# A hybrid encoder block on one Trainium2 core: backward GLA contributions copied by VectorE, the last head's second norm and the MLP's low parts placed later

## The chip, the core and the metric

The kernel runs on one core of one Trainium2 chip. The metric is the device time of one execution in microseconds. Five engines work side by side, each through its own queue in order: TensorE (PE; its weight loads are shown as PEld), VectorE (DVE), ScalarE (ACT), GpSimd (POOL) and SyncE (SP), which issues most DMA transfers. TensorE accumulates in PSUM, where the kernel keeps four pairs of tiles (banks) of 128 x 512 float32 values, tagged "mm", "s", "o" and "t".

## The reference

One encoder layer on 1024 tokens of width 1024, in float32:

```python
n = rmsnorm(h, ln_mix_g)
proj = n @ w_in                      # q/k/v for attention, q/k/v/r and decay factors for GLA
y_na = neighbourhood_attention(...)  # 8 heads x 64, window 8 x 16 on a 16 x 64 grid, softmax with bias
y_gla = bidirectional_gla(...)       # 4 heads, chunks of 64 tokens, forward + backward state
h = h + concat([y_na, y_gla]) @ w_out
h = h + square(relu(rmsnorm(h, ln_ff_g) @ w1)) @ w2
return rmsnorm(h, ln_final_g)
```

For each GLA head a chunk contributes k^T v to a state in each direction; the states of the 16 chunks follow from the contributions by a scan, `S = decay * S + contribution`, forward in 64 partitions and backward in the other 64. The output of a head is the sum of a product within the chunk (masked scores times v) and a product of the decayed q with the state. It is then normed over the head's 128 values and multiplied by a gate.

## The kernel before

All activations lie transposed, features in partitions, in two halves of 512 tokens (`hf`). Float32 products are made of float32r parts: a value is split into a high part (a rounded copy by ScalarE) and a low part (value minus high part, a subtraction), and a product is three matmuls: high x high, high x low, low x high.

The stages follow each other: the input's norm and first projections; four GLA heads; attention in four pairs of heads (`p`), each in eight column blocks (`b`); the output projection; the MLP in four chunks of the hidden width, of which the first is done plainly (`FirstPlain`, `SecondPlain`) and the next by seven products of sums of blocks (`First`, `Second`, Strassen's scheme); the last chunk together with the final norm. Projections that a later stage needs are cut into steps of three matmuls (`Fill`), which are put between the parts of GLA and attention by tables of step counts (`GLA_FILL`, `NA_FILL`), so that TensorE has work while the other engines prepare. Their weights come by SP (`wf`); ScalarE makes a negated copy, a DMA from POOL's queue adds the weights to it (`wl`), and ScalarE casts the high part (`wh`).

The order on each engine is a static one. A scheduler orders instructions by dependencies, priorities (`tc.high_priority`) and its own estimate of times. `tc.keep_in_program_order` (`kp` in the MLP) pins an instruction behind all that was traced before on its engine. In the MLP all is pinned, so the code's order is the engines' order.

*A GLA head* (lines 670 to 693). `gla_contrib` (L569) makes the contributions of eight chunks into two banks tagged "s" and copies them to the state tile `st`: the forward half, partitions 0 to 63, by L583, the backward half, partitions 64 to 127, by L586, both on ScalarE; that is four copies for each of two calls. `gla_scan` runs the scan on VectorE, L606 forward and L609 backward, first steps 1 to 7 (not pinned), then 8 to 11 behind `gla_within(h, 0)`, then 12 to 14 behind `gla_within(h, 1)`. `gla_within` makes the scores within the chunks into two "s" banks (of two in all) and copies them masked by VectorE (L600). `gla_gates` of the next head uses "s" banks too (tile `la`). `gla_norm` (L629) norms one half: a sum over partitions by TensorE into a "t" bank, then in `rstd_from` Ln, Exp, Identity and Square on ScalarE (L230, L231, L237, L238) and two steps on VectorE (L239, L240), then the gate (L635) and the head's output (L636), which still lies in an "o" bank.

*The start of attention* (L890 to L897). The bias of the first pair is loaded and masked (`bias_for`, `masked`, L771), eight steps of filler run, then `softmax(0, 0)` is made: scores into two "s" banks, per head of the pair an addition of the bias with a maximum on VectorE (L825), an exponential with its sum on ScalarE (L827), a reciprocal and a scaling on VectorE (L829, L830). `softmax` of the next block needs the same two banks. `turn` transposes the result (L120, tile `pt`).

*The first MLP products.* `prepare(k)` queues, ahead of product k, what is due: the high and low part of the weights of product k + 2 (`prep2`), the activation of product k - 1 (`acts`), and jobs from a table. Products 0 to 7 work on the first token half, 8 to 15 on the second, 16 on are the second matmul. The jobs make the normed input of the second half (`normed`, L1377, eight values at products 2 to 7) and the sums of blocks that the later chunks need (`sums123`, L1386, at products 8 to 15; `sum4`, L1398, at 33 to 40). `put` (L1369) splits a value: a rounded copy on ScalarE (L1371), then the low part on VectorE (`low`, L1056). `whole` (L1365) adds high and low part on GpSimd.

Of the kernel before, what the change touches and what calls it, by code (L numbers as in the profile page):

```python
# [18 lines left out]
P = 128  # L19
# [48 lines left out]
def block_kernel(ctx, tc, xT, g_mix, w_in, w_z, rpb, na_mask, gu, gb, g_gla, sel_f, sel_b,  # L68
# [390 lines left out]
    with pool("gla", R) as gp:  # L459
# [110 lines left out]
        def gla_contrib(h, kt, st, hf):  # L570
            cb = [bank("s", f"c{h}_{hf}_{i}") for i in range(2)]
            for i in range(8):
                n = hf * 8 + i
                o = 64 * (n % 2)
                PE.matmul(cb[n % 2][:, (i // 2) * P:(i // 2 + 1) * P],
                          kt[o:o + 64, n // 2, :], vtok[h][o:o + 64, n // 2, :],
                          start=True, stop=True)
            for par in range(2):
                src = cb[par].rearrange("p (a b) -> p a b", a=4)
                n0 = hf * 8 + par  # L580

                k = 4 if n0 + 7 < NCH else 3
                S.copy(st[0:64, n0 + 1:n0 + 2 * k:2, :], src[0:64, 0:k, :])  # L583

                k = 0 if n0 > 0 else 1
                S.copy(st[64:128, n0 - 1 + 2 * k:n0 + 6:2, :], src[64:128, k:4, :])  # L586

        def gla_within(h, hf, qD, kI):

# [39 lines left out]
        def gla_norm(h, hf, ob, sq):  # L629
            c = slice(hf * H, (hf + 1) * H)  # L630
            v = bank("t", f"ov{h}_{hf}")
            PE.matmul(v, ones, sq, start=True, stop=True)
            r = rstd_from(v, 1.0 / P, gp, "n", H, "g1", 2)
            if (h, hf) in gated:
                V.tensor_tensor(r, yg[h][:, c], r, op=ALU.mult)  # L635
            V.tensor_tensor(yg[h][:, c], r, ob, op=ALU.mult)  # L636
            normed.add((h, hf))
# [22 lines left out]
        for h in range(GH):  # L660
# [12 lines left out]
            gla_scan(dec, st, 1, NCH // 2)  # L673
            fill.at(GLA_FILL, h, 3)
            gla_within(h, 0, qD, kI)
            gla_scan(dec, st, NCH // 2, NCH - 4)
            fill.at(GLA_FILL, h, 4)
            gla_within(h, 1, qD, kI)
            gla_scan(dec, st, NCH - 4, NCH - 1)
            fill.at(GLA_FILL, h, 5)  # L680
            if h + 1 < GH:
                bs[h + 1] = gla_gates(h + 1)
# [7 lines left out]
            fill.at(GLA_FILL, h, 9)  # L690
            gla_norm(h, 0, ob[0], sq[0])
            fill.at(GLA_FILL, h, 10)
            gla_norm(h, 1, ob[1], sq[1])
        bias_rows(range(ROWS))
        fill.run()
    gla_stack.close()
# [38 lines left out]
    with soon("na") as ap, soon("qkv") as qp:  # L735
# [154 lines left out]
        qt = lambda: qp.tile([P, H], F32, tag="qt", name="qt", bufs=2)  # L890
        qk = qk_tiles(0)
        fill.add(na_v(0), ("v", 0))
        with tc.high_priority(offset=SOON_B):
            bt = bias_for(0)
        fill.run(NA_PRE)
        xs = softmax(0, 0, *qk, bt)
        masked(bt, (5, 0))  # L897
        for p in range(NH // 2):
            if p > 1:
# [273 lines left out]
    class Second(Stage):  # L1173
# [61 lines left out]
        def add(self, p, j, o, s):  # L1235
            for d, c0 in {1: ((j, 0),), 5: ((j + 4, H),), 6: ((j, H),), 3: ((j, H),),
                          7: ((j + 4, H),), 2: ((j, 0),), 4: ((j + 4, 0),)}[p]:
                c = slice(c0 + s.start, c0 + s.stop)
                kp(V.tensor_tensor(hT[:, d, c], hT[:, d, c], o[:, s], op=ALU.add))  # L1239

    class FirstPlain(Stage):

        order = [((hf, m), kh) for hf in range(2) for m in range(4) for kh in range(2)]

        def __init__(self, c):
            self.w, self.u, self.parts = Weights(w1[c], ("A11", "A12", "A21", "A22")), {}, {}

        def prep2(self, p, kh):
            self.parts[p, kh] = self.w.low(self.w.high(f"A{p[1] // 2 + 1}{kh + 1}", p[1] % 2))

        def mm(self, p, kh):
            (hf, m), w = p, self.parts.pop((p, kh))
# [114 lines left out]
        kp(G.tensor_tensor(dst, h.bitcast(F32), l.bitcast(F32), op=ALU.add))  # L1367

    def put(key, k, x):  # L1369
        h, l = place(key, k)  # L1370
        kp(S.copy(h, x))  # L1371
        low(l, x, h, V)

    b = {}

    def normed(key, k):
        c = {"B12": 0, "B22": 1}[key]  # L1377
        if k == 0 and "S" not in b:
            b["S"] = mu.tile([P, D], F32, tag="S", name="b0")
        b[key, k] = t = (b["S"][:, c * H:(c + 1) * H] if k == 0 else  # L1380
                         mp.tile([P, H], F32, tag=("uh", "ul")[c], name=f"b{c}{k}", bufs=3))
        kp(V.scalar_tensor_tensor(t, hT[:, 4 * c + k, H:T], gff[:, 4 * c + k:4 * c + k + 1], r1,
                                  op0=ALU.mult, op1=ALU.mult))
        put(key, k, t)

    def sums123(k, step):  # L1386
        b12, b22 = b["B12", k], b["B22", k]
        if step == 0:
            b["B11", k] = ub("b11")
            whole(b["B11", k], "B11", k)  # L1390
            kp(V.tensor_tensor(b22, b22, b12, op=ALU.subtract))
            put("T3", k, b22)
        else:
            kp(V.tensor_tensor(b12, b12, b["B11", k], op=ALU.subtract))
            kp(V.tensor_tensor(b22, b22, b["B11", k], op=ALU.add))
            put("T1", k, b12)
            put("T2", k, b22)

    def sum4(k, step):
        if step == 0:  # L1400
            b["x", k] = x = [mp.tile([P, H], F32, tag=tag, name=f"b4{k}", bufs=3) for tag in ("uh", "ul")]
            whole(x[0], "B21", k)
            whole(x[1], "T2", k)
        else:
            x = b["x", k]
            kp(V.tensor_tensor(x[0], x[0], x[1], op=ALU.subtract))
            put("T4", k, x[0])

    for n, k in enumerate((2, 3, 3, 4, 5, 5, 6, 7)):
        job(k, normed, ("B12", "B22")[n // 4], n % 4)  # L1410
    for n, k in enumerate((1, 2, 3, 0)):
        for step in range(2):
            job(8 + 2 * n + step, sums123, k, step)
    for k in range(4):
        for step in range(2):
            job(33 + 2 * k + step, sum4, k, step)

    f2 = SecondPlain(0, f1.u)
    stage(f2)
# [165 lines left out]
```

## Time and profile before

| | |
|---|---|
| time, median of 3 runs | 1180.3 us (1179.51 to 1181.38) |
| the profiled execution | 1180.51 us |
| its span, first to last instruction | 1178.6 us |
| TensorE busy | 1149.7 us, 98% |
| VectorE busy | 862.7 us, 73% |
| ScalarE busy | 664.8 us, 56% |
| GpSimd busy | 241.6 us, 21% |
| mean granted clock of TensorE | 0.990 |

Busy time is the time in which an engine has an instruction in work. [...] In a timeline, the number in brackets is how long the engine stood idle before the instruction, and behind the arrow stands what it waited for.

### The profile page before, as it was taken

To read this page: it belongs to the slowest core of one execution; us is meant where nothing else is said; L and a number is where in the kernel's file an instruction comes from. 1 tells how busy PE (TensorE), PEld (TensorE's weight loads), DVE (VectorE), ACT (ScalarE), POOL (GpSimd) and SP (SyncE) were. 2 spreads that over 40 slices of the span, in tenths; PEclk is the share of its full clock that TensorE was granted. 3 is DMA by queue.
4 is the path that set the end of the run, shared out by engine and by line. 5 is a ranking of instruction groups with operands and counts; after the bars stand their busy time and mean duration, and the time that the engine had idled before them with its cause. 6 is when DMAs were issued, how large, how long until landed. Compare 5 with 4: busy or idle time off the path is not lost.

```text
span 1178.6 us, 15430 instructions
## 1 busy us (share of the span) xinstructions
PE 1149.7 (98%) x5632; PEld 945.6 (80%) x5632; DVE 862.7 (73%) x1565; ACT 664.8 (56%) x1222; POOL 241.6 (21%) x199
## 2 busy tenths in 40 slices
PE   8999899999999999999999999999999999999996
PEld 8878788767887878887788888888888888888876
DVE  8777868766767785686858875967859768587455
ACT  6767566656666665455634636446355463453665
POOL 5200000202021123510003320402304114032005
PEclk8999999989999999999999999999999999999998
DMA  7333132322324252320211112111211122111204
GB/s 241 76 86 94 41 72 46 87 69 55 80 45 100 68 179 73 107 107 8 82 54 36 54 54 72 37 55 54 72 66 31 50 69 72 54 37 54 72 1 143
DMA packets 40283, 84.03 MB, mean 71 GB/s; under 512 B 9264, under 2 KB 20656, under 8 KB 40208
## 3 DMA queue, kind: packets, MB, share of 16 engines
q1 hardware_dynamic: 36608, 71.11, 18.1%
q0 software_dynamic: 3456, 11.94, 5.8%
q8 instruction: 44, 0.72, 0.2%
q14 instruction: 31, 0.25, 0.1%
q10 hardware_dynamic: 144, 0.00, 0.0%
HBM read 78.85 MB, written 5.96 MB: 72 GB/s over the span
## 4 chain that ended last, share of the span: by engine, by line
PE 83%; DVE 7%; ACT 6%; issue 1%; DMA 1%; SPq 0%; DVEq 0%; ACTq 0%
PE f L115 26%; PE u L115 24%; PE proj L115 15%; PE op L115 7%; PE sc L115 2%; PE no L115 2%; PE o L115 1%; PE pt L120 1%; PE sb L115 1%; PE ob L115 1%; PE z L115 1%; PE a L115 1%; DMA wl<-in_w_in 1%; PE c L115 1%; PE opl L115 0%
## 5 line engine op out<-in xcount | busy, mean ns | idle before, releaser
L1079 ACT CAST ph<-A 128x512 fp32r<-128x512 f32 x166 | 102.9, 621 | 146.5 <-PE f L115 73.6
L1057 POOL TENSOR_TENSOR ul<-uB,uh 128x512 fp32r<-128x512 f32 x84 | 109.1, 1317 | 330.5 <-ACT uh L1092 213.4
L115 PE MATMUL f<-uh,ph 128*128 128x512 f32 x400 | 155.9, 390 | 2.1 <-ACT u L1100 1.4
L115 PE MATMUL f<-ul,ph 128*128 128x512 f32 x400 | 155.8, 390 | 0.1
L115 PE MATMUL f<-uh,pl 128*128 128x512 f32 x400 | 155.8, 389 | 0.0
L1057 DVE TENSOR_TENSOR pl<-A,ph 128x512 fp32r<-128x512 f32 x166 | 112.7, 688 | 52.6 <-ACT ph L1079 52.6
L115 PE MATMUL proj<-nh,wh 128*128 128x512 f32 x352 | 151.1, 429 | 0.0
L115 PE MATMUL proj<-nh,wl 128*128 128x512 f32 x352 | 139.4, 396 | 1.4 <-DMA wl<-in_w_in 1.4
L115 PE MATMUL proj<-nl,wh 128*128 128x512 f32 x352 | 138.9, 395 | 0.0
L1239 DVE TENSOR_TENSOR hT<-hT,f 128x512 f32<-128x512 f32 x168 | 113.0, 687 | 19.8 <-PE f L115 19.6
L115 PEld LDWEIGHTS f<-uh,ph 128*128 128x128 f32 x400 | 75.1, 188 | 18.4 <-ACT u L1100 1.8
L115 PEld LDWEIGHTS f<-ul,ph 128*128 128x128 f32 x400 | 75.1, 188 | 16.0 <-DVE ul L1057 0.4
L115 PEld LDWEIGHTS f<-uh,pl 128*128 128x128 f32 x400 | 75.1, 188 | 15.6
L115 PE MATMUL u<-n,ph 128*128 128x512 f32 x288 | 85.2, 391 | 0.0
L115 PEld LDWEIGHTS proj<-nh,wh 128*128 128x128 f32 x352 | 67.2, 191 | 18.2 <-issue 5.6
L1092 ACT CAST uh<-uB 128x512 fp32r<-128x512 f32 x84 | 51.9, 618 | 51.1 <-PE f L115 33.0
L115 PEld LDWEIGHTS proj<-nh,wl 128*128 128x128 f32 x352 | 66.8, 190 | 16.9 <-DMA wl<-in_w_in 1.8
L115 PE MATMUL u<-T,ph 128*128 128x512 f32 x256 | 77.0, 390 | 0.2 <-ACT ph L1079 0.2
L115 PEld LDWEIGHTS proj<-nl,wh 128*128 128x128 f32 x352 | 67.2, 191 | 11.7 <-issue 1.7
L115 PE MATMUL op<-y,wh 128*128 128x512 f32 x240 | 75.6, 396 | 0.4 <-DVE y L714 0.4
L115 PE MATMUL u<-nt,ph 128*128 128x512 f32 x224 | 69.0, 389 | 0.0
L827 ACT ACTIVATE xsc<-xsc,sm 128x384 f32<-128x384 f32 (+1 forms) x64 | 37.3, 584 | 51.3 <-DVE sm L825 51.1
(302 smaller groups left out, 2469.6 us busy)
## 6 DMA issues: line engine op xcount, KB each, us to landing
A<-in_w SPq DMA_DIRECT2D x64, 512.0 KB
wf<-in_w_in SPq DMA_DIRECT2D x22, 512.0 KB
wl<-in_w_in POOLq DMA_DIRECT2D x21, 512.0 KB, 6.7
wf<-in_w_out SPq DMA_DIRECT2D x17, 512.0 KB
hT<-in_xT SPq DMA_DIRECT2D x2, 2048.0 KB
xs<-in_xT SPq DMA_DIRECT2D x6, 512.0 KB
out<-hT SPq DMA_DIRECT2D x4, 512.0 KB
out<-hT SPq DMA_DIRECT2D x8, 256.0 KB
```

The source lines that it names most:

```text
L115: m = nc.tensor.matmul(*args, **kw)
L120: tc.keep_in_program_order(nc.tensor.transpose(*args, **kw))
L827: S.activation(x[:, :n], x[:, :n], AF.Exp, scale=-1.0, bias=sm[:, i, 0:1], accum_out=sm[:, i, 1:2])
L1057: return kp(eng.tensor_tensor(l, x, h.bitcast(F32), op=ALU.subtract))
L1079: kp(S.copy(ph, x))
L1092: kp(S.copy(uh, x))
L1239: kp(V.tensor_tensor(hT[:, d, c], hT[:, d, c], o[:, s], op=ALU.add))
```

## The change

In `gla_contrib` the copy of the backward half goes from ScalarE to VectorE. In the head's loop `gla_scan` now runs steps 8 and 9 before the second `gla_within`, and 10 to 14 behind it. For the last head the second `gla_norm` isn't called; its sum over partitions stays, its ScalarE steps are traced ahead of the bias load of attention, into tiles of attention's pool (`qc`, `qt`), and its four VectorE steps behind `softmax(0, 0)`, the first of them pinned there.

In the MLP low parts are no longer subtracted at once: `put`, and `prep2` of `FirstPlain` from product 2 on, note them in a list, and `settle` subtracts what is owed, after the next value has been made. The jobs of `normed` and `sums123` start one product earlier, in part, and go through k = 0, 1, 2, 3. `sums123` no longer calls `whole`: it subtracts the high and the low part one after the other on VectorE, and T2 is made from T1.

```diff
--- before.py
+++ after.py
@@ -583,7 +583,7 @@
                 S.copy(st[0:64, n0 + 1:n0 + 2 * k:2, :], src[0:64, 0:k, :])
 
                 k = 0 if n0 > 0 else 1
-                S.copy(st[64:128, n0 - 1 + 2 * k:n0 + 6:2, :], src[64:128, k:4, :])
+                V.tensor_copy(st[64:128, n0 - 1 + 2 * k:n0 + 6:2, :], src[64:128, k:4, :])
 
         def gla_within(h, hf, qD, kI):
 
@@ -673,10 +673,10 @@
             gla_scan(dec, st, 1, NCH // 2)
             fill.at(GLA_FILL, h, 3)
             gla_within(h, 0, qD, kI)
-            gla_scan(dec, st, NCH // 2, NCH - 4)
+            gla_scan(dec, st, NCH // 2, NCH // 2 + 2)
             fill.at(GLA_FILL, h, 4)
             gla_within(h, 1, qD, kI)
-            gla_scan(dec, st, NCH - 4, NCH - 1)
+            gla_scan(dec, st, NCH // 2 + 2, NCH - 1)
             fill.at(GLA_FILL, h, 5)
             if h + 1 < GH:
                 bs[h + 1] = gla_gates(h + 1)
@@ -690,7 +690,13 @@
             fill.at(GLA_FILL, h, 9)
             gla_norm(h, 0, ob[0], sq[0])
             fill.at(GLA_FILL, h, 10)
-            gla_norm(h, 1, ob[1], sq[1])
+            if h + 1 < GH:
+                gla_norm(h, 1, ob[1], sq[1])
+            else:
+                v_last = bank("t", "ovlast")
+                PE.matmul(v_last, ones, sq[1], start=True, stop=True)
+                o_last = ob[1]
+                assert (h, 1) in gated
         bias_rows(range(ROWS))
         fill.run()
     gla_stack.close()
@@ -890,10 +896,22 @@
         qt = lambda: qp.tile([P, H], F32, tag="qt", name="qt", bufs=2)
         qk = qk_tiles(0)
         fill.add(na_v(0), ("v", 0))
+
+        ly = qp.tile([P, T], F32, tag="qc", name="ly")[:, 0:H]
+        lt, lu = qt(), qt()
+        S.activation(lt, v_last, AF.Ln, bias=epsb, scale=LNSH / P)
+        S.activation(ly, lt, AF.Exp, bias=expb, scale=-0.5)
+        S.activation(lu, v_last, AF.Identity, bias=epsn, scale=-0.5 / P)
+        S.activation(lt, ly, AF.Square)
         with tc.high_priority(offset=SOON_B):
             bt = bias_for(0)
         fill.run(NA_PRE)
         xs = softmax(0, 0, *qk, bt)
+        tc.keep_in_program_order(V.tensor_tensor(lt, lt, lu, op=ALU.mult))
+        V.scalar_tensor_tensor(ly, lt, 1.5, ly, op0=ALU.add, op1=ALU.mult)
+        c = slice(H, T)
+        V.tensor_tensor(ly, yg[GH - 1][:, c], ly, op=ALU.mult)
+        V.tensor_tensor(yg[GH - 1][:, c], ly, o_last, op=ALU.mult)
         masked(bt, (5, 0))
         for p in range(NH // 2):
             if p > 1:
@@ -1238,15 +1256,24 @@
                 c = slice(c0 + s.start, c0 + s.stop)
                 kp(V.tensor_tensor(hT[:, d, c], hT[:, d, c], o[:, s], op=ALU.add))
 
+    owed = []
+
     class FirstPlain(Stage):
 
         order = [((hf, m), kh) for hf in range(2) for m in range(4) for kh in range(2)]
+        late_lows = False
 
         def __init__(self, c):
             self.w, self.u, self.parts = Weights(w1[c], ("A11", "A12", "A21", "A22")), {}, {}
 
         def prep2(self, p, kh):
-            self.parts[p, kh] = self.w.low(self.w.high(f"A{p[1] // 2 + 1}{kh + 1}", p[1] % 2))
+            ph, x = self.w.high(f"A{p[1] // 2 + 1}{kh + 1}", p[1] % 2)
+            pl = mp.tile([P, H], F32R, tag="pl", name="pl", bufs=3)
+            self.parts[p, kh] = ph, pl
+            if self.late_lows:
+                owed.append((pl, x, ph))
+            else:
+                low(pl, x, ph, V)
 
         def mm(self, p, kh):
             (hf, m), w = p, self.parts.pop((p, kh))
@@ -1367,9 +1394,14 @@
         kp(G.tensor_tensor(dst, h.bitcast(F32), l.bitcast(F32), op=ALU.add))
 
     def put(key, k, x):
+
         h, l = place(key, k)
         kp(S.copy(h, x))
-        low(l, x, h, V)
+        owed.append((l, x, h))
+
+    def settle():
+        while owed:
+            low(*owed.pop(0), V)
 
     b = {}
 
@@ -1381,23 +1413,29 @@
                          mp.tile([P, H], F32, tag=("uh", "ul")[c], name=f"b{c}{k}", bufs=3))
         kp(V.scalar_tensor_tensor(t, hT[:, 4 * c + k, H:T], gff[:, 4 * c + k:4 * c + k + 1], r1,
                                   op0=ALU.mult, op1=ALU.mult))
+        settle()
         put(key, k, t)
 
     def sums123(k, step):
         b12, b22 = b["B12", k], b["B22", k]
+        h, l = place("B11", k)
         if step == 0:
-            b["B11", k] = ub("b11")
-            whole(b["B11", k], "B11", k)
+            x = ub("t3")
+            kp(V.tensor_tensor(x, b22, b12, op=ALU.subtract))
+            settle()
+            put("T3", k, x)
+            kp(V.tensor_tensor(b12, b12, h.bitcast(F32), op=ALU.subtract))
+        else:
+            kp(V.tensor_tensor(b12, b12, l.bitcast(F32), op=ALU.subtract))
+            settle()
+            put("T1", k, b12)
             kp(V.tensor_tensor(b22, b22, b12, op=ALU.subtract))
-            put("T3", k, b22)
-        else:
-            kp(V.tensor_tensor(b12, b12, b["B11", k], op=ALU.subtract))
-            kp(V.tensor_tensor(b22, b22, b["B11", k], op=ALU.add))
-            put("T1", k, b12)
+            settle()
             put("T2", k, b22)
 
     def sum4(k, step):
         if step == 0:
+            settle()
             b["x", k] = x = [mp.tile([P, H], F32, tag=tag, name=f"b4{k}", bufs=3) for tag in ("uh", "ul")]
             whole(x[0], "B21", k)
             whole(x[1], "T2", k)
@@ -1406,14 +1444,17 @@
             kp(V.tensor_tensor(x[0], x[0], x[1], op=ALU.subtract))
             put("T4", k, x[0])
 
-    for n, k in enumerate((2, 3, 3, 4, 5, 5, 6, 7)):
+    f1.late_lows = True
+    for n, k in enumerate((2, 2, 3, 3, 4, 5, 5, 6)):
         job(k, normed, ("B12", "B22")[n // 4], n % 4)
-    for n, k in enumerate((1, 2, 3, 0)):
+    for k in range(4):
         for step in range(2):
-            job(8 + 2 * n + step, sums123, k, step)
+            job(7 + 2 * k + step, sums123, k, step)
+    job(15, settle)
     for k in range(4):
         for step in range(2):
             job(33 + 2 * k + step, sum4, k, step)
+    job(41, settle)
 
     f2 = SecondPlain(0, f1.u)
     stage(f2)
```

## Rows read from the trace of the kernel before

**Rows 1.** The page, part 1: busy us, share of the span, instructions.

```profile
PE 1149.7 (98%) x5632; PEld 945.6 (80%) x5632; DVE 862.7 (73%) x1565; ACT 664.8 (56%) x1222; POOL 241.6 (21%) x199
```

**Rows 2.** Stretch, its us; busy us of PE, PEld, DVE, ACT, POOL; PEclk; DMA share, GB/s.

```profile
115.00:128.00 13.00, 11.26 (x80) 8.55 (x78) 8.29 (x19) 9.87 (x16) 0.86 (x1) 0.97 0.39 97
128.00:140.00 12.00, 10.53 (x51) 7.85 (x52) 9.96 (x23) 3.82 (x7) 0.00 (x0) 0.90 0.17 49
250.00:265.00 15.00, 12.12 (x43) 8.47 (x42) 11.59 (x32) 6.85 (x16) 0.86 (x1) 0.77 0.32 69
548.00:585.00 37.00, 33.53 (x140) 25.55 (x139) 30.43 (x46) 24.87 (x44) 3.07 (x2) 1.00 0.21 68
```

**Rows 3.** The chain that ended last, one full-pace piece: start, us, what.

```profile
621.96 38.09 PE u L115 x168
```

**Rows 4.** Timeline of head 1: start, us, engine, line, instruction, idle before.

```profile
121.48 2.62 DVE L606 SCALAR_TENSOR_TENSOR st<-st,dec 64x128 f32<-64x128 f32 x7
...
124.15 0.58 ACT L583 COPY st<-c 64x512 f32<-64x512 f32 x1
...
125.37 0.48 PE L115 MATMUL a<-qD,kI 64*128 64x128 f32 x2 [1.14 <-ACT st L586]
...
126.44 2.67 DVE L609 SCALAR_TENSOR_TENSOR st<-st,dec 64x128 f32<-64x128 f32 x7 [2.34 <-ACT st L586]
...
132.22 0.72 DVE L600 COPY_PREDICATED asb<-selB,a 128x512 f32<-128x512 uint32 x1
...
133.09 1.12 PE L115 MATMUL a<-qD,kI 64*128 64x128 f32 x14 [0.54 <-DVE asb L600]
...
136.65 0.50 PE L115 MATMUL la<-zT,guh 128*128 128x512 f32 x1 [0.82 <-DVE asb L600]
```

**Rows 5.** The tile st, one line of it: durations in ns.

```profile
L583 ACT COPY st<-c x16: 472/578/582, 75.3 to 221.9; 64x512 f32<-64x512 f32 x12, 64x384 f32<-64x384 f32 x4
```

**Rows 6.** Timeline of head 2, last masked copy and second scores products.

```profile
178.09 0.73 DVE L600 COPY_PREDICATED asb<-selB,a 128x512 f32<-128x512 uint32 x1
...
179.05 1.16 PE L115 MATMUL a<-qD,kI 64*128 64x128 f32 x16
```

**Rows 7.** Timeline of the change from GLA to attention.

```profile
249.32 0.69 ACT L230 ACTIVATE nt<-ov,small 128x512 f32<-128x512 f32 x1 [0.82 <-DVE nt L239]
...
251.31 0.69 DVE L804 TENSOR_TENSOR vT<-proj,rms 128x512 f32<-128x512 f32 x1
...
252.91 0.69 DVE L239 TENSOR_TENSOR nt<-nt,nu 128x512 f32<-128x512 f32 x1 [0.91 <-ACT nt L238]
...
253.78 0.39 PE L115 MATMUL proj<-nh,wl 128*128 128x512 f32 x1
...
255.09 0.69 DVE L636 TENSOR_TENSOR yg<-ny,o 128x512 f32<-128x512 f32 x1
...
256.37 0.42 DVE L825 CUSTOM_DVE_ANT_0 xsc<-sc,bt 128x256 f32<-128x256 f32 x1
...
256.85 0.69 PE L115 MATMUL sc<-k00p,q 128*128 128x384 f32 x1 [2.67 <-DVE sm L825]
...
264.39 0.34 PE L115 MATMUL sc<-k00p,q 128*128 128x384 f32 x1
```

**Rows 8.** The page, part 6: one DMA issue, KB, us to landing.

```profile
wl<-in_w_in POOLq DMA_DIRECT2D x21, 512.0 KB, 6.7
```

**Rows 9.** Timeline of the MLP's first products.

```profile
547.93 1.77 PEld L115 LDWEIGHTS u<-n,ph 128*128 128x128 f32 x8
...
555.94 1.28 DVE L1057 TENSOR_TENSOR B<-b,B 128x512 fp32r<-128x512 f32 x1 [0.68 <-ACT B L1371]
...
574.95 0.69 DVE L1057 TENSOR_TENSOR nt<-b,nt 128x512 fp32r<-128x512 f32 x1
...
575.55 0.69 DVE L1057 TENSOR_TENSOR pl<-A,ph 128x512 fp32r<-128x512 f32 x1
...
582.87 0.19 PEld L115 LDWEIGHTS f<-uh,ph 128*128 128x128 f32 x1 [1.79 <-ACT u L1100]
```

## The prediction

> **What bounds the kernel now.** I read the busy times first. TensorE is busy 1149.7 of 1178.6 us [rows 1], so only time in which TensorE stands still, or runs at its lower clock, can be won. To find that time I read busy time by stretches and kept the stretches that the diff touches [rows 2]: the reader is to see 1.74 and 1.47 us of TensorE idle around head 1 of the gated linear attention (GLA) with a granted clock of 0.97 and 0.90, 2.88 us idle at clock 0.77 where GLA hands over to neighbourhood attention, and 3.47 us idle at full clock in the first MLP products. Then the timeline of each stretch says who was late. The chain of waits gives the undisturbed pace: 168 matmuls in 38.09 us, 0.2267 us each [rows 3]. All else is filled, so a change outside these stretches is worth nothing unless it opens a new hole.
>
> **Part 1, GLA contributions and scan.** In each contribution two banks are read by two copies each, all four on ScalarE at 0.58 us [rows 5]. The change gives two of the four to VectorE: per head 4 x 0.58 = 2.3 us leave ScalarE. No VectorE copy of such a slice stands in the trace. Its bounds: ScalarE's 0.58 [rows 5] and VectorE's 0.69 for a two-input step out of PSUM of the same width (the line of tile vT) [rows 7]. I take 0.69, the same engine, so 2.8 us per head are added to VectorE. [...]
>
> Head 1 is the only head with a hole worth naming. Its bound: idle 1.74 + 1.47 = 3.2 us, and clock 13 x 0.03 + 12 x 0.10 = 1.6 us, together 4.8 [rows 2]. What happens there [rows 4]: the first four scores products wait for banks that ScalarE, busy with weight casts, frees late (copies from 124.15, products at 125.37); VectorE waits 2.34 us and starts its backward scan at 126.44; the second products wait for the masked copy that starts at 132.22; and the next head's gate matmul waits 0.82 us at 136.65 for the masked copies behind it. After: VectorE's queue shows no wait in its row at 121.48, so the first two copies push that scan by 1.4 us; its 2.62 us and two more copies end at 121.48 + 1.4 + 2.62 + 1.4 = 126.9, against 126.44 today. So VectorE, now waiting for nothing, begins the backward scan no earlier, and the second products still start near 133. What TensorE gains in front of them is lost waiting for them: price nothing. The rest is the reordered scan: the masked copies of the second half come after two steps instead of four. Two steps are four instructions of 2.62 / 7 = 0.37 us, 1.5 us; the wait of 0.82 goes and a little beyond. I take **1.3 us**, with bounds of -1.0 (the 0.5 us of lateness seen twice) and 4.8. Heads 0, 2 and 3: nothing, covered by projections that run between the parts; without that cover they lose as head 1 does (last rival).
>
> **Part 2, the last head's second norm.** Today ScalarE starts the second norm at 249.32 after 0.82 us of waiting for a buffer of the first. Four VectorE steps follow, 252.91 to 255.09 + 0.69 = 255.78, then masks, and the first maximum at 256.37. TensorE had finished its filler at about 254.0 and waited 2.67 us for that maximum, which frees the scores bank [rows 7]. The clock then fell: 15 x 0.23 = 3.4 us, with 2.88 us idle 6.3 us at most [rows 2]. [...] The ScalarE steps use new buffers and run in the 249 to 253 gap; VectorE's four steps are pinned behind the scaling of the first maxima and stand between it and the second block's scaling. VectorE is busy 11.59 of the 15 us [rows 2], so with all its work still inside, the stretch shrinks by 3.4; with the four steps slipping past it, by up to 6.3. The next late thing is a weight transfer: its cast sits on ScalarE behind the first exponential, and it needs 6.7 us from issue to landing [rows 8]. It moves with the first maximum, 256.37 - 252.6 = 3.8 us, and TensorE takes the next block soon after 264.39. I take **3.8 us**. The low bound is 0.9: 3.8 less the 2.9 us of the four steps, should these stand before the second maxima. The output bank and the sum's bank stay taken longer; their next users are attention's outputs and transposes, later than the steps. No DMA moves; SyncE's queue is passed by no new instruction.
>
> **Part 3, the MLP's low parts.** Today VectorE makes a value, waits for ScalarE's rounded copy, subtracts, and only then takes the next. From the weight load at 547.93 to the one at 582.87 lie 10 products of 12 matmuls and 9 more: 129 x 0.2267 = 29.24 us against 34.94, so 5.7 us are lost [rows 3, 9]. At 555.94 one subtraction took 1.28 us beside GpSimd's whole-value sum instead of the 0.69 of its line [rows 9]; those sums go. After: subtractions run one operation later, so VectorE waits for no copy, and all jobs start one product earlier. Its work per two products in the sums grows from 8 steps to 9. Independent steps start 0.60 us apart (574.95, 575.55) [rows 9]; one dependent pair adds 0.1: 9 x 0.60 + 0.1 = 5.5 us, against 24 x 0.2267 = 5.44 on TensorE. It falls behind 0.1 us per pair, 0.3 in all, and each part is wanted two products (5.4 us) later, so nothing is late. I take **5.5 us**; bounds 2.6 and 5.7. The lower one: if steps don't overlap, 9 x 0.69 = 6.2 us per pair, 0.77 too long, four pairs 3.1 us. [...] Against it stand the two rows 0.60 apart. Releasing raw weights later delays loads by a step or two; DMA is at 0.21 of its time there [rows 2]. The one-later subtraction in the fourth sums meets a stretch at full pace [rows 3]: nothing.
>
> **Sum.** 1.3 + 3.8 + 5.5 = 10.6 us. The profiled execution took 1180.51 us (1178.6 of span and 1.9 around it), 0.2 above the median of 1180.3. TensorE is the chain from 583 us on, so what is won before arrives at the end: 1180.5 - 10.6 = **1169.9 us**.
>
> **Rivals.** *VectorE becomes the bound* (0.20): part 1 gives nothing, the norm's steps precede the second maxima (0.9), steps don't overlap (2.6): 3.5 us, **1177.0**. For it: 11.59 of 15 us, and 30.43 of 37 us in the MLP [rows 2]; against it: the 0.60 us spacing. [...] *The norm isn't out of the way* (0.07): its new buffers lie in space that GLA still uses, so ScalarE's steps start late ahead of the first exponential; 10.6 - 3.8 = 6.8, **1173.7**. *All holes close* (0.06): 4.8 + 6.3 + 5.7 = 16.8, **1163.7**. *Nothing comes through* (0.08): the reordered queues open equal holes in attention, **1180**. *Slower* (0.07): VectorE's copies delay the masked copies in heads 0, 2 and 3 too, TensorE waits at the second products, and the clock falls as in head 1: 3 x 4.8 = 14.4 lost, part 1 gives nothing, parts 2 and 3 give 9.3: 5.1 longer, **1185.6**. It decides in head 2, where the masked copy ends at 178.82 and the product starts at 179.05: 0.2 us of room [rows 6]. Against it: ScalarE's copies, which VectorE awaits today, end earlier when halved.
>
> **How the numbers follow.** The forecast has 0.52. The range runs from 1163.5 to 1177.0: it takes in all but "nothing" and "slower" (0.15). A measurement of this kernel tells 0.2% (2.4 us) from no change; faster are the forecast and the first three rivals, 0.85; same 0.08; slower 0.07.
>
> **What would show it.** Right: no idle at the second block's scores near 254, clock 1.00 from 250 to 265; all products from 537 to 590 spaced 2.72 us; the gate matmul in head 1 without wait, and the second products still waiting. Wrong: waits of TensorE for masked copies in heads 0, 2 or 3; VectorE's idle at zero with TensorE waiting on low parts; a wait for a weight transfer above 1 us near 261; a clock below 1 in a stretch that is full today.

## The result, and the profile after

The changed kernel takes 1170.36 us (median, 1170.14 to 1170.92) against 1179.9 us for the kernel before, measured beside it: a ratio of 0.992, with an interval of 0.9908 to 0.9932. The forecast was 1169.9 us. The profiled execution of the changed kernel took 1170.14 us, its span is 1168.4 us.

The page's busy times and the windows of the stretches in [rows 1] and [rows 2], after (columns as there):

```profile
PE 1143.7 (98%) x5632; PEld 943.9 (81%) x5632; DVE 868.9 (74%) x1585; ACT 654.3 (56%) x1206; POOL 232.5 (20%) x195
```

```profile
115.00:128.00 13.00, 11.38 (x75) 8.59 (x76) 10.61 (x20) 7.89 (x13) 0.85 (x1) 1.00 0.34 79
128.00:140.00 12.00, 10.91 (x72) 8.83 (x70) 11.14 (x28) 4.70 (x9) 0.00 (x0) 1.00 0.31 83
250.00:265.00 15.00, 12.76 (x64) 9.53 (x64) 12.76 (x38) 6.87 (x16) 0.86 (x1) 1.00 0.32 72
548.00:585.00 37.00, 37.00 (x164) 30.61 (x164) 26.91 (x44) 21.40 (x37) 0.00 (x0) 1.00 0.26 85
```

The granted clock of TensorE (PEclk: a share of full speed, the mean over the stretch) stands at 1.00 in all four, and the MLP stretch holds 164 matmuls instead of 140. In GLA and at its handover TensorE still idles 1.62, 1.09 and 2.24 us. VectorE's busy time rose by 6.2 us, ScalarE's fell by 10.5.

Where the time went is read from the starts of the same instructions in both traces: the transposes of head 0's keys, the last head's first product of q with the state, the first run of 120 matmuls of the output projection, and the first full-pace piece of the chain [rows 3].

| from, to | before, us | after, us | gain | forecast |
|---|---|---|---|---|
| transposes, head 0, to last head's state product | 168.97 | 168.24 | 0.73 | 1.3 |
| on to the output projection's 120 matmuls | 262.72 | 258.43 | 4.29 | 3.8 |
| on to the first piece of 168 matmuls | 120.93 | 115.31 | 5.62 | 5.5 |

Their sum is 10.6 us, as forecast, but not all of it was won by the change. The trace of the kernel before is one execution, in which the clock fell in head 1 (0.97, 0.90) and at the handover from GLA to attention (0.77) [rows 2]. Of the kernels below, some have the same instructions there as the kernel before, and their clock stayed at 1.00. In two of them the first stage takes 167.92 us (the norm's part alone) and 167.76 us (late low parts alone), no longer than the 168.24 us of the changed kernel. In two the second stage takes 261.97 us (VectorE's copies alone) and 261.91 us (late low parts alone), 3.5 us more than the 258.43 us after. So with the clock up on both sides part 1 wins nothing and part 2 wins 3.5 us; the 0.73 us and the other 0.8 of the 4.29 us are what the fallen clock cost in that one execution. In part 3 the clock is 1.00 on both sides. The last piece of the chain, VectorE's final six steps, starts 10.69 us earlier (1172.83 to 1162.14), but the span is only 10.2 us shorter: between that start and the end lie 5.8 us before and 6.3 after. No step of the change stands there, and this was not pursued.

**Head 0 and head 1 after.** From the timeline: start, us, engine, line, instruction, idle before.

```profile
76.44 0.69 DVE L471 TENSOR_TENSOR vtmp<-proj,rms 128x512 f32<-128x512 f32 x1
77.16 0.69 DVE L586 COPY st<-c 64x512 f32<-64x512 f32 x1
77.91 1.16 PE L115 MATMUL c<-vtok,kt 64*128 64x128 f32 x14 [0.96 <-DVE st L586]
...
80.53 1.30 DVE L586 COPY st<-c 64x512 f32<-64x512 f32 x2
...
121.65 1.41 DVE L293 SCALAR_TENSOR_TENSOR qd<-proj,rms 64x512 f32<-64x512 f32 x2
122.98 0.69 DVE L586 COPY st<-c 64x512 f32<-64x512 f32 x1
123.72 1.16 PE L115 MATMUL c<-vtok,kt 64*128 64x128 f32 x14 [0.87 <-DVE st L586]
...
126.35 1.30 DVE L586 COPY st<-c 64x512 f32<-64x512 f32 x2
...
127.68 2.67 DVE L609 SCALAR_TENSOR_TENSOR st<-st,dec 64x128 f32<-64x128 f32 x7
...
133.31 1.13 PE L115 MATMUL a<-qD,kI 64*128 64x128 f32 x14 [1.09 <-DVE asb L600]
...
135.86 0.40 PE L115 MATMUL la<-zT,guh 128*128 128x512 f32 x1
```

In both heads a copy stands behind another VectorE instruction (L471, L293) that has nothing to do with it, and TensorE waits for the bank at the second contributions. Head 0's last two copies start at 80.53, behind seven scan steps (L606, 77.88 to 80.50). In head 1 the second scores products start at 133.31 (133.09 before), and the gate matmul at 135.86 no longer waits [rows 4].

**GLA to attention after.** The same view:

```profile
249.19 0.64 ACT L905 ACTIVATE qt<-ly 128x512 f32<-128x512 f32 x1
...
252.08 0.42 DVE L831 CUSTOM_DVE_ANT_0 xsc<-sc,bt 128x256 f32<-128x256 f32 x1
...
252.54 0.51 ACT L833 ACTIVATE xsc<-xsc,sm 128x256 f32<-128x256 f32 x1 [2.71 <-DVE sm L831]
...
253.05 1.04 ACT L175 ACTIVATE wl<-wf 128x1024 fp32r<-128x1024 f32 x1
...
253.19 0.33 PE L115 MATMUL sc<-k00p,q 128*128 128x384 f32 x1
...
254.39 0.86 POOL L176 DMA_DIRECT2D wl<-in_w_in  x1 [21.74 <-PE sc L115]
...
256.20 0.68 DVE L910 TENSOR_TENSOR qt<-qt 128x512 f32<-128x512 f32 x1
...
256.43 0.41 PE L120 MATMUL pt<-ident,xsc 128*128 128x128 f32 x2 [1.24 <-DVE xsc L836]
...
261.28 0.50 PE L115 MATMUL proj<-nh,wl 128*128 128x512 f32 x1 [1.00 <-DMA wl<-in_w_in]
```

The first maximum starts at 252.08 (256.37 before) and the second block's scores follow at 253.19 without a wait, where they had waited 2.67 us [rows 7]. Two waits stand behind, 1.24 us for VectorE's second scaled tile and 1.00 us for the weight transfer. They are not new. The kernel with VectorE's copies alone has the old order here and its clock stayed at 1.00 from 250 to 265 us; TensorE's waits from 247 to 268 us in it (waited for: us, times, longest):

```profile
PE sc L115 <- DVE sm L825: 2.7, 1, 2.7
PE pt L120 <- DVE sm L829: 1.6, 1, 1.6
PE proj L115 <- DMA wl<-in_w_in: 1.0, 1, 1.0
```

In the kernel before only 0.2 us of the second and nothing of the third show, while the clock stood at 0.77 in the mean. In the changed kernel the transfer is issued at 254.39, behind its cast (253.05), which stands behind the first exponential (252.54), while ScalarE had been idle for 2.71 us.

**The MLP after.** VectorE's steps of one pair of products, same view:

```profile
549.51 0.68 DVE L1424 TENSOR_TENSOR t<-b,b 128x512 f32<-128x512 f32 x1
550.11 0.69 DVE L1075 TENSOR_TENSOR nt<-b,nt 128x512 fp32r<-128x512 f32 x1
...
551.32 0.68 DVE L1427 TENSOR_TENSOR b<-b,n 128x512 f32<-128x512 f32 x1
552.03 0.69 DVE L1429 TENSOR_TENSOR b<-b,n 128x512 f32<-128x512 f32 x1
...
555.05 0.69 DVE L1424 TENSOR_TENSOR t<-b,b 128x512 f32<-128x512 f32 x1
```

No row carries a wait. Nine steps take 5.54 us (549.51 to 555.05); independent steps start 0.60 us apart, the one dependent pair (551.32, 552.03) 0.71.

### The profile page after: what moved, and what is told of

The parts are those of the page before. It is cut to its first block, busy times and chain, and to the rows that moved or that the text cites. A ratio compares the mean times of both kernels' runs of the same rounds, so it can differ in the third digit from the quotient of the medians.

```text
span 1168.4 us, 15410 instructions
## 1 busy us (share of the span) xinstructions
PE 1143.7 (98%) x5632; PEld 943.9 (81%) x5632; DVE 868.9 (74%) x1585; ACT 654.3 (56%) x1206; POOL 232.5 (20%) x195
## 4 chain that ended last, share of the span: by engine, by line
PE 85%; DVE 7%; ACT 5%; DMA 2%; issue 1%; SPq 0%; DVEq 0%; ACTq 0%
PE f L115 27%; PE u L115 25%; PE proj L115 14%; PE op L115 7%; PE no L115 2%; PE sc L115 2%; PE o L115 1%; PE pt L120 1%; DMA wl<-in_w_in 1%; PE sb L115 1%; PE ob L115 1%; DVE st L606 1%; PE a L115 1%; DVE st L586 1%; PE z L115 1%
## 5 line engine op out<-in xcount | busy, mean ns | idle before, releaser
L115 PEld LDWEIGHTS u<-n,ph 128*128 128x128 f32 x288 | 54.0, 188 | 11.7 <-issue 0.5
```

Of the source, the lines that this page charges most:

```text
L115: m = nc.tensor.matmul(*args, **kw)
```

## The experiments

The three parts were first made singly, then part 1 was divided, then the steps of parts 2 and 3 were tested. Each edit is one to the kernel before or to the changed kernel, as said; each ratio is to the kernel before, run beside it.

**VectorE's copies alone** (kernel before, L586):

```diff
-                S.copy(st[64:128, n0 - 1 + 2 * k:n0 + 6:2, :], src[64:128, k:4, :])
+                V.tensor_copy(st[64:128, n0 - 1 + 2 * k:n0 + 6:2, :], src[64:128, k:4, :])
```

> The kernel before with the backward copies on VectorE and nothing else. My theory (the copies give nothing, VectorE's queue takes back what ScalarE saves): the second half's copies of a head stand behind seven scan steps, so the first scores product of head 0 comes 0.9 us later and head 1 gains about that much because the clock stays up: 1180 us, between 0.5 us longer and 0.5 us shorter than before. Rival (ScalarE's lateness was the price, the copies are what part 1 earns): 0.8 to 2 us shorter, and the gate matmul of head 1 at 136.65 us comes 1 us or more earlier.

Measured: 1180.92 us against 1180.38, ratio 1.0005 (0.9996 to 1.0014): nothing that can be told from zero. The waits of TensorE from head 0's contributions to the end of GLA (waited for: us, times, longest):

```profile
PE c L115 <- DVE st L586: 1.8, 2, 1.0
PE proj L115 <- DMA wl<-in_w_in: 1.4, 1, 1.4
PE a L115 <- DVE asb L600: 1.1, 1, 1.1
PE la L115 <- DVE asb L600: 0.8, 1, 0.8
```

The clock in head 1 was 1.00 in both stretches, but the wait of 0.8 us at the gate matmul stayed, and 1.8 us for VectorE's copies came in. Against the norm's part alone, where the clock stayed up too, the last head's first state product comes 2.0 us later (169.87 and 167.92 us behind head 0's transposes).

**The divided scan alone** (kernel before):

```diff
-            gla_scan(dec, st, NCH // 2, NCH - 4)
+            gla_scan(dec, st, NCH // 2, NCH // 2 + 2)
...
-            gla_scan(dec, st, NCH - 4, NCH - 1)
+            gla_scan(dec, st, NCH // 2 + 2, NCH - 1)
```

> The kernel before with the scan split after two steps instead of four and nothing else. My theory (this is where part 1 earns): the wait of 0.82 us at the gate matmul of head 1 goes, 1.0 to 1.3 us shorter, 1179.1 us; the clock falls around 126 us as before. Rival (the copies earn): within 0.3 us of before.

Measured: 1178.63 us, ratio 0.9986 (0.9976 to 0.9995). By the times that is 1.75 us shorter than the kernel before; in its trace the gain up to the last state product is 0.7 to 0.8 us, in an execution in which the clock fell deeper in head 1 (0.93 and 0.79). The wait at the gate matmul is gone. So the divided scan shortens the kernel by itself, as forecast.

**VectorE's copies in head 1 alone** (changed kernel):

```diff
-                V.tensor_copy(st[64:128, n0 - 1 + 2 * k:n0 + 6:2, :], src[64:128, k:4, :])
+                (V.tensor_copy if h == 1 else S.copy)(st[64:128, n0 - 1 + 2 * k:n0 + 6:2, :], src[64:128, k:4, :])
```

> The changed kernel with the backward copies on VectorE in head 1 alone, on ScalarE in heads 0, 2 and 3. Theory (the copies cost 0.9 us in head 0 and 0.4 us in head 3, where they stand behind the scan, and pay only in head 1, where ScalarE is late with weight casts and the clock fell): 1.0 to 1.3 us shorter than the changed kernel, 1169.2 us. Rival (the copies pay in every head): longer than the changed kernel.

Measured: 1168.89 us (1168.44 to 1169.05), ratio 0.9905 (0.989 to 0.992): 1.5 us below the changed kernel (1.8 by the starts of the last piece, 1162.14 and 1160.38). By the starts in the traces, relative to head 0's transposes, the heads come out like this:

| gain on the kernel before, us, at | changed kernel | copies in head 1 alone |
|---|---|---|
| head 0, second scores products | -0.99 | 0.00 |
| head 1, first state product | 1.17 | 2.17 |
| head 2, first state product | 1.14 | 2.17 |
| head 3, first state product | 0.73 | 2.16 |

The difference of the columns is the price of the copies: head 0 loses 1.0 us by them, head 2 nothing, head 3 0.4. The level of both columns from head 1 on is not the change's alone, since about 1 us of it is the fallen clock of the one execution of the kernel before (168.97 us against 167.92 and 167.76 to the last head's state product). Against the norm's part alone, which has the old head 1 at clock 1.00, head 1's first state product comes 1.2 us earlier (72.48 and 73.71 us behind head 0's transposes). How much of that is the scan's and how much the copies' is not shown: the divided scan with parts 2 and 3 and no copy on VectorE was not run. The single gains of the scan, the norm and the MLP (1.75, 4.4 and 5.2 us) would put that kernel near 1169 us as well, by a rough estimate from their medians.

**VectorE's copies twice** (changed kernel; each of the 16 copies is made a second time into the same place):

> The changed kernel with each of VectorE's copies of the backward contributions made twice: 16 more steps of 0.69 us, 11.0 us more on VectorE, nothing less on ScalarE. Theory (the copies cost where TensorE soon waits for the masked copies that stand behind them: head 0 lost 0.9 us and head 3 0.4, head 2 next to nothing, and four copies put 2.8 us in each head): the next 2.8 us per head find no room either: 1 to 2.8 us per head, 4 to 11 us in all, 1174 to 1181, and with the clock below 1 in some head above that. Rival (the fill of projections takes the copies up, and the 0.9 in head 0 came from the order in its queue, not from VectorE's load): under 2 us.

Measured: 1179.76 us against 1180.08, ratio 0.9999 (0.9988 to 1.0009): 9.4 us more than the changed kernel for 16 copies, 0.59 each; all that parts 2 and 3 earn is gone. The waits as above, and the second window of head 1:

```profile
PE c L115 <- DVE st L587: 6.1, 8, 1.5
...
PE a L115 <- DVE asb L601: 1.4, 2, 1.0
PE a L115 <- DVE st L587: 0.7, 2, 0.5
```

```profile
128.00:140.00 12.00, 10.73 (x67) 8.35 (x68) 11.18 (x25) 2.29 (x5) 0.31 (x1) 0.87 0.45 97
```

TensorE waits for a contributions bank eight times, and the clock is below 1 again, at 0.87. The rival "slower" is like this only in part: it had TensorE waiting for the masked copies, and those are 1.4 us here against 6.1 us for the banks that VectorE's copies hold. With 2.8 us of copies a head two heads lose 1.0 and 0.4 us; with 5.5 us a head the four heads lose 9.0 us more by the trace.

**The last head's second norm alone** (kernel before, with the diff's lines from L693 to the four VectorE steps):

> The kernel before with the last head's second norm moved and nothing else. My theory (the wait of 2.67 us for the first maximum and the fall of the clock behind it go, the weight transfer is next late): 3.8 to 4.3 us shorter, 1176.3 us, granted clock 1.00 from 250 to 265 us. Rival (VectorE is full there, 11.59 of 15 us, and the moved steps come back ahead of the second maxima): 0.9 us shorter, 1179.4 us.

Measured: 1175.98 us, ratio 0.9958 (0.9943 to 0.9973): 4.4 us. By the starts in the trace its own stretch is 3.87 us shorter (262.72 to 258.85), and 3.1 us against the two kernels with the old order whose clock stayed up. TensorE's waits from 248 to 266 us:

```profile
PE pt L120 <- DVE xsc L836: 1.3, 1, 1.3
PE proj L115 <- DMA wl<-in_w_in: 1.1, 1, 1.1
```

They are the two of the changed kernel, and the wait of 2.67 us is gone: this part does not need the others.

**The next block's weights at a higher priority** (changed kernel):

```diff
-        with tc.high_priority(offset=SOON_W):
+        with tc.high_priority(offset=soon):
...
-            parts[BLOCKS[n]] = weights(w_in[BLOCKS[n]])
+            parts[BLOCKS[n]] = weights(w_in[BLOCKS[n]], soon=1000 if BLOCKS[n] == 13 else SOON_W)
```

> The changed kernel with one weight cast (the low part of block 13) given a higher priority, so that ScalarE makes it in its idle 2.7 us ahead of the first exponential near 250 us. Theory (that transfer is the next late thing in the second part): TensorE's wait of about 1 us near 260 us goes, 0.8 to 1.2 us shorter than the changed kernel. Rival (VectorE is next late right behind it): under 0.3 us.

Measured: 1170.14 us, ratio 0.9916 (0.9899 to 0.9932), as the changed kernel. This tells nothing of the theory: the priority did not move the cast, which stands at 252.67 behind the exponential at 252.16, and the wait for the transfer is 1.35 us.

**The first block's exponentials pinned** (changed kernel, `softmax`):

```diff
-                S.activation(x[:, :n], x[:, :n], AF.Exp, scale=-1.0, bias=sm[:, i, 0:1],
-                             accum_out=sm[:, i, 1:2])
+                e = S.activation(x[:, :n], x[:, :n], AF.Exp, scale=-1.0, bias=sm[:, i, 0:1],
+                                 accum_out=sm[:, i, 1:2])
+                if p == b == 0:
+                    tc.keep_in_program_order(e)
```

> The changed kernel with the two exponentials of the first block pinned, so that ScalarE's two weight casts (wl, wh) stand ahead of them instead of between them. In the trace of the changed kernel ScalarE stands idle from 249.8 to 252.5 us, the casts take 1.04 and 1.03 us, and the weight transfer is issued at 254.39, behind the cast that ends at 254.09. Theory (the weight transfer is next late because its cast waits for the first exponential): the cast starts near 250, the transfer is issued about 3 us earlier, TensorE's wait of 1.00 us for it goes, and the kernel is 0.8 to 1.5 us shorter than the changed one, near 1169. The wait of 1.24 us for the second scaled tile stays or moves, since VectorE now scales both tiles behind the second block's maxima. Rival (VectorE is next late): what TensorE doesn't wait for the transfer it waits for VectorE, less than 0.3 us in all.

Measured: 1168.89 us (1168.82 to 1169.53), ratio 0.9907 (0.9893 to 0.9922): 1.5 us below the changed kernel (1.2 by the starts of the last piece, 1162.14 and 1160.93). Its timeline:

```profile
249.68 1.06 ACT L175 ACTIVATE wl<-wf 128x1024 fp32r<-128x1024 f32 x1
...
251.03 0.86 POOL L176 DMA_DIRECT2D wl<-in_w_in  x1 [18.42 <-ACT wl L175]
...
252.50 0.51 ACT L833 ACTIVATE xsc<-xsc,sm 128x256 f32<-128x256 f32 x1 [0.83 <-DVE sm L831]
...
255.99 0.87 PE L120 MATMUL pt<-ident,xsc 128*128 128x128 f32 x4 [1.06 <-DVE sm L837]
```

The cast fills ScalarE's idle time, the exponential starts no later than before (252.50 against 252.54), the transfer is issued 3.4 us earlier, and TensorE's wait for it is gone. The wait for the scaled tiles stays, 1.06 us. That TensorE waited for this transfer because its cast stood behind the exponential is thereby shown.

**The two gains together** (copies in head 1 alone, and the pinned exponentials):

> The kernel with VectorE's copies in head 1 alone (1168.89 us, 1.25 below the changed kernel) and the two pinned exponentials together. If the two gains lie in different places and don't touch, they add: 1167.4 to 1168.1 by the theory of the weight transfer, 1168.6 to 1168.9 by its rival.

Measured: 1167.63 us (1167.23 to 1167.81), ratio 0.9896 (0.988 to 0.9913). By the medians the two gains of 1.5 us come to 2.7 together; by the starts of the last piece 1.76 and 1.21 us come to 2.99 us, so they add. This version is shorter than both kernels.

**The MLP's part alone** (kernel before, with the diff's lines from L1240 on):

> The kernel before with the MLP's part of the change and nothing else. My theory (VectorE no longer waits for each rounded copy): all products from 537 to 590 us evenly spaced, 5.5 to 5.7 us shorter, 1174.8 us. Rival (part of the gain was made by the earlier parts of the change, which shift the MLP against its transfers): under 4.5 us.

Measured: 1175.19 us, ratio 0.9951 (0.9936 to 0.9966): 5.2 us. From the output projection to the chain's first full piece the trace has 115.30 us, as in the changed kernel (115.31).

**Low parts subtracted at once** (changed kernel; sums, earlier jobs and VectorE's subtractions stay):

```diff
-        owed.append((l, x, h))
+        low(l, x, h, V)
...
-    f1.late_lows = True
```

> The changed kernel, but each low part is subtracted at once behind its rounded copy; the sums without GpSimd and the jobs one product earlier stay. Theory 1 (the wait of VectorE for each rounded copy is the price): VectorE waits about 0.7 us per value again, with 9 steps per two products it falls behind by more than before, and most of the 5.6 us returns: 3 to 6 us longer than the changed kernel. Theory 2 (GpSimd's sums, which stretched VectorE's subtractions to 1.28 us, and the later start were the price): within 1 us of the changed kernel.

Measured: 1182.23 us, ratio 1.0021 (1.001 to 1.0032): 11.9 us more than the changed kernel. VectorE's timeline:

```profile
557.75 0.69 DVE L1075 TENSOR_TENSOR T<-b,T 128x512 fp32r<-128x512 f32 x1 [0.69 <-ACT T L1399]
...
559.72 0.69 DVE L1075 TENSOR_TENSOR nt<-b,nt 128x512 fp32r<-128x512 f32 x1 [0.68 <-ACT nt L1399]
...
562.30 0.69 DVE L1075 TENSOR_TENSOR nt<-t,nt 128x512 fp32r<-128x512 f32 x1 [0.68 <-ACT nt L1399]
...
565.49 0.69 DVE L1075 TENSOR_TENSOR T<-b,T 128x512 fp32r<-128x512 f32 x1 [0.69 <-ACT T L1399]
```

Three waits of 0.68 us a pair make its period 7.74 us (557.75 to 565.49) instead of 5.54, above TensorE's 5.44. Four pairs cost 8.8 us of the 12.6 by which the stretch from the output projection to the chain's first full piece is longer (127.88 us). Over the stretch TensorE waits 5.0 us for high parts of weights, and the clock was 0.86 between 560 and 572 us; how the other 3.8 us divide was not settled. In the kernel before a pair of the sums has one such wait and takes 5.76 us (557.75 to 563.51). So the new sums and earlier jobs without the late subtractions lose more than parts 1 and 2 earn.

**Late low parts alone, with the old sums** (the subtractions settled one operation later; `whole` on GpSimd, the order and the due products of the jobs as before; one `settle` ahead of each sum and a last job that settles):

> The changed kernel with the low parts one operation later, but the sums as before (whole values by GpSimd, jobs at their old products and in their old order). Theory 1 (the wait for each copy is the price): 0 to 1.5 us longer than the changed kernel. Theory 2 (GpSimd and the later start): 3 us longer or more.

This run was built on the kernel before, without parts 1 and 2, though its expectation speaks of the changed one; so it is compared with the MLP's part alone. Measured: 1175.3 us, ratio 0.9958 (0.9943 to 0.9974), against 1175.19 there; by the trace its stretch is 1.5 us longer (116.78 against 115.30). The same edits on the changed kernel:

> The changed kernel with late low parts, but with the old sums: GpSimd adds the whole values, the jobs stand where they stood, and the sums are made in the old order. The same edit on the kernel before gave 1175.3, against 1175.19 for the whole third part there, with a stretch 1.5 us longer by its landmarks. Theory (late subtractions carry the third part, the earlier jobs and GpSimd's leaving give 1 to 1.5 us): 1170.3 to 1171.9. Rival (GpSimd's sums are as much of it): over 1173.

Measured: 1170.84 us (1170.53 to 1171.14), ratio 0.9923 (0.9903 to 0.9943), 0.5 us above the changed kernel. In its trace one subtraction beside GpSimd's sum is stretched, and TensorE waits once, for the activation behind the sums:

```profile
556.57 1.78 DVE L1075 TENSOR_TENSOR nt<-b,nt 128x512 fp32r<-128x512 f32 x1
...
572.99 0.50 PE L115 MATMUL f<-uh,ph 128*128 128x512 f32 x1 [1.14 <-ACT u L1118]
```

VectorE's waits for rounded copies of `put` from 527 to 592 us, first in the kernel before, then in this run (normed values T and B, sums nt):

```profile
DVE nt L1057 <- ACT nt L1371: 2.7, 4, 0.7
DVE B L1057 <- ACT B L1371: 2.7, 4, 0.7
DVE T L1057 <- ACT T L1371: 2.8, 4, 0.8
```

```profile
DVE nt L1075 <- ACT nt L1399: 2.1, 3, 0.7
```

The late subtraction takes away the eight waits at the normed values. In the old sums three waits stay, and a pair of products still takes VectorE 5.76 us (548.82 to 554.58). By the starts in the traces the late subtraction gives 4.2 of part 3's 5.6 us, and the new sums and earlier jobs the last 1.5 (0.5 by the medians).

## Why the prediction was right

**The bound.** This was right: TensorE's busy share stayed at 98%, and what was won in the three stretches came through to the last piece of the chain (10.69 us). The forecast of 10.6 us was added up from waits and had the clock in its upper bounds alone. That the starts in the two traces also give 10.6 is in part luck: near 2 us of it is the fallen clock of the profiled execution of the kernel before (168.97 us against 167.92 and 167.76 in the first stage, 262.72 against 261.97 and 261.91 in the second). With the clock up on both sides the parts give about 0, 3.5 and 5.6 us. By the medians the kernel is 9.5 us shorter, and the parts made singly give 1.2 (copies and scan: -0.5 and 1.75), 4.4 and 5.2 us, 10.8 in all. How often the clock of the kernel before falls was not counted, so the medians can't be divided further.

**Part 1, 1.3 us forecast, 0.7 measured in these two executions, nothing with the clock up.** The price of a copy, forecast at 0.69 us, was right: the 16 copies have a median of 0.689 us, and those of 384 values take 0.560. In head 1 the mechanism was right. (One reading was off: only the first two matmuls of the scores start at 125.37 [rows 4], the other 14 wait a further 0.60 us for the second bank, until 126.46; nothing in the sum hangs on it.) The backward scan, forecast at 126.9, starts at 127.68, behind 1.0 us of delay from head 0; the second products still wait (1.09 us), and the gate matmul's wait went. The start of the second products at 133.31, "still near 133", is chance, since head 0's delay is in it. But without that delay (copies in head 1 alone) they come 0.3 us later than in the norm's part alone, where the clock stayed up: 63.10 and 62.83 us behind head 0's transposes. So the copies do gain nothing in front of them, and the 1.2 us of head 1 are near the forecast's 1.3. The step that failed is "Heads 0, 2 and 3: nothing, covered by projections". Head 0 lost 1.0 us and head 3 0.4, as the run with the copies in head 1 alone shows. In head 0 copies that ScalarE made at once now stand behind VectorE's evacuation (L471) and seven scan steps. The low bound of -1.0 had held a loss of this size, but in head 1.

**Part 2, 3.8 forecast, 4.3 measured, 3.5 with the clock up.** The first maximum was forecast 3.8 us earlier, at 252.6, the author's estimate from [rows 7] (251.31 + 0.69 for the bank of tile vT, then 0.6 us of masks). The trace of the changed kernel shows not 252.6 but 252.08, 4.3 us earlier than before (256.37), of which 0.8 had been won ahead of this stage (the last head's first state product, 238.31 to 237.50), so 3.5 here; the wait of 2.67 us went. The clock stayed at 1.00, as in all nine profiled kernels with the norm moved. That it fell to 0.77 in the kernel before because of that wait is not shown: two kernels with the old order have the same wait of 2.7 us and a clock of 1.00. "The next late thing is a weight transfer" is right in part. Its issue moved with the first maximum, by 4.3 us (258.67 to 254.39), and taking its cast out from behind the exponential gave a further 1.2 to 1.5 us. But TensorE's first wait after the change is the 1.24 us for VectorE's second scaled tile, which the prediction did not have; in the kernel before it showed as 0.2 us. The norm's own steps stand behind that tile (L910 at 256.20), so they are not its cause. The wait for the transfer, 1.00 us, is at the limit that the prediction set as a sign of error.

**Part 3, 5.5 forecast, 5.6 measured.** The pair's period was forecast at 9 x 0.60 + 0.1 = 5.5 us and is 5.54; the 37 us from 548 to 585 are full. That VectorE's waits for the rounded copies were the price is shown by the runs with the subtractions at once and with the old sums. The rival by which steps don't overlap falls: independent steps of 0.68 and 0.69 us start 0.60 us apart (549.51, 550.11).

**The rivals.** VectorE did not become the bound: it was busy 12.76 of 15 us and 26.91 of 37. "Slower" did not come; part of what it feared came in heads 0 and 3, 1.4 us in place of its 14.4, and at twice the copies TensorE waited for contribution banks more than for masked copies. Of the 16.8 us of "all holes close" 10.6 came; 4.1 of the missing ones are part 1's, 2.0 part 2's.

## What to carry to other kernels

Before an operation goes to an engine with free time, look at what stands in that engine's queue where the operation would be made, not at its mean load: the copies cost 1.4 us in two heads where they came to stand behind VectorE's other steps, and leaving them on ScalarE there made the kernel 1.5 us shorter. Where a value is split by one engine and finished by another, let the second make the next value first; here that takes away a wait of 0.7 us at each of eight normed values, and with the new sums three in each pair of products. When a wait goes, ask at once which cast or load is queued behind the thing that moved: an idle engine with the next transfer's cast behind a waiting instruction was worth another 1.2 to 1.5 us. Before a gain is read from two traces, compare the granted clocks of the stretch, and look for another run with the same instructions and the clock up.

## What was not expected of the hardware

In head 1 of the kernel before, the same instructions in the same order ran with different clocks. The windows of two kernels whose head 1 is that of the kernel before, first the norm's part alone, then the MLP's part alone (the kernel before: 0.97 and 0.90 [rows 2]):

```profile
128.00:140.00 12.00, 9.96 (x57) 7.54 (x56) 10.55 (x24) 5.21 (x9) 0.00 (x0) 1.00 0.13 38
```

```profile
128.00:140.00 12.00, 11.07 (x53) 8.27 (x52) 10.20 (x25) 4.28 (x8) 0.00 (x0) 0.86 0.18 52
```

Ahead of it TensorE had stood idle 1.75 us of 13 in one and 1.74 in the other. So the clock of 0.97 and 0.90 in these short stretches of one profiled execution is not a cost that each execution pays (1.00 in both with the norm's part alone), and the 1.6 us that the forecast's upper bound took from it is only that one execution's. The handover shows the same: from 250 to 265 us five kernels with the old order have 0.77, 0.77, 0.89, 1.00 and 1.00, all with the wait of 2.7 us. With VectorE's copies in head 1, made once, the clock was 1.00 there in all eight profiled executions of eight kernels. What decides it was not tested.

A subtraction of two float32 inputs on VectorE, 0.69 us by itself, took 1.28 us beside GpSimd's sum in the kernel before [rows 9] and 1.78 us in the run with the old sums. Not each one beside such a sum is stretched: in that run two took 0.68 us each (543.33 and 543.93) beside a sum that itself took 2.81 us (from 542.95).
